# GpSimd takes 48 of the low-part subtractions from VectorE in a transformer block on one core

## Chip, cores and metric

The kernel runs on one core of one Trainium2 chip. The metric is the device time of one execution in microseconds (us); three executions were timed and the median is quoted. A further execution was taken with the hardware profiler, and all rows below come from it.

## What is computed

One block of a streaming encoder for 512 tokens of width 2048, in float32. The first half is attention (latent attention and stick-breaking attention, merged by gates). The second half, where the change lies, is an expert retrieval:

```
h  = rmsnorm(x) * (1 + scale) + shift                 # 512 x 2048
q  = (h @ w_q) -> 8 heads x 256                       # query weights
s1, s2 = q's two halves against 128 keys each
v1, i1 = top_k(s1, 16);  v2, i2 = top_k(s2, 16)       # per head
sc, ci = top_k(v1[i] + v2[j], 16)                     # of 256 pairs
idx = e1 * 128 + e2;  g = softmax(sc)                 # 16 experts a head
act = gelu(h . u_tab[idx]);  y = sum(g * act * v_tab[idx])
x  = x + gate * y
```

## The kernel before, in words

**Split products.** TensorE multiplies in a reduced float32 format (fp32r). To keep accuracy, each weight tile of 128x1024 is split by the helper hl (line 100): the tile raw is loaded on SyncE's queue, ScalarE copies it to hi in fp32r (line 110), VectorE forms lo = raw - hi (line 111), and mm3 (line 124) makes three products, hi*hi (line 125), hi*lo of the activations (line 126) and lo*hi (line 127). There are four raw buffers and three each of hi and lo. After the second normalization the flag prio is set (line 772), so that every later call of hl takes the first branch (lines 109 to 111), which gives the two instructions a high priority.

**Order.** The instructions of each engine run in a fixed order, which a planner makes from its own estimate of durations, with the order of the program as priority. Each engine takes its instructions strictly in that order.

**The stage of the change (build3).** The query product goes head by head: wq_part (line 774) makes a quarter of a head's product, so 4 tiles and 96 matmuls a head. Heads 0 and 1 come first (lines 784 to 786 and 900 to 903). Then, for each head, ScalarE copies the product (qT, line 825), TensorE makes the scores (pscore, line 836), ScalarE copies these (s, line 839, four buffers), the product of the next head is issued (wq_mm), and VectorE selects the best keys (topk, line 843): rows of top-8, index and replace operations over 128 and then 256 candidates, small conversions (lines 851, 863, 864, 867), the candidate sums (cand, line 855), then one-hot compares, products and reductions (lines 869 to 871), a difference df (line 873) whose exponential ScalarE takes (line 874), and the weights gn (line 878).

After the heads come 12 chunks of the dense first product of the experts (lead_chunk, line 889, through u_mm, line 880): a chunk is 2 tiles and 48 matmuls of 352 columns into the tile pul, and ScalarE takes a gelu of it (line 893). These do not need the selection. What follows does: the indices (line 936), a rearranged copy h2r with one buffer (line 948) which TensorE transposes (ph2x, line 951), and the transposes of the selected indices and weights (ptr, line 1009). Then 12 further chunks (line 1042) are interleaved with g_batch (line 1018): 44 batches in which VectorE builds one-hot tiles o1 and o2 (lines 1026 and 1028) and TensorE multiplies them (pg, line 1034). From there GpSimd also issues the gathers of expert rows (line 964), and VectorE uses the rows (lines 970 and 982). The rest of the kernel, half of its time, runs the remaining chunks of the first product and the second product (pvv).

GpSimd does nothing else than a few memsets early (line 549) until the writes of g_d (line 1039) and the gathers.

Of the kernel before, what the change touches and what calls it, by code (L numbers as in the profile page):

```python
# [24 lines left out]
NL0 = 12  # L25
# [47 lines left out]
def build(tc, a, dbg=None, upto=99):  # L73
    nc = tc.nc
    VE, SC, GP, TE, SY = nc.vector, nc.scalar, nc.gpsimd, nc.tensor, nc.sync
# [21 lines left out]
    def bank(name="bk"):  # L97
        return ps.tile([128, 512], F32, name=name, tag="ps", bufs=8)

    def hl(src, n=1024, rb=4, sb=3, q=None):  # L100
        raw = st.tile([128, 1024], F32, name="raw", tag="raw", bufs=rb)
        hi = st.tile([128, 1024], F32R, name="hi", tag="hi", bufs=sb)
        lo = st.tile([128, 1024], F32R, name="lo", tag="lo", bufs=sb)
        if q is None:
            SY.dma_start(raw[:, :n], src)
        else:
            q.dma_start(raw[:, :n].rearrange("p (m c) -> p m c", m=src.shape[1]), src)
        if prio[0]:
            with tc.high_priority():
                SC.activation(hi[:, :n], raw[:, :n], AF.Copy)  # L110
                VE.tensor_sub(lo[:, :n], raw[:, :n], hi[:, :n])  # L111
        else:
            SC.activation(hi[:, :n], raw[:, :n], AF.Copy)  # L113
            VE.tensor_sub(lo[:, :n], raw[:, :n], hi[:, :n])  # L114
        return hi, lo
# [163 lines left out]
    def part_mm(src, m0, m1, k0, k1, out, begin, end):  # L279
        nk = k1 - k0  # L280
        pb = {}
        for ma in range(m0, m1, max(1, 8 // nk)):
            mb = min(m1, ma + max(1, 8 // nk))
            parts = -(-nk // 8)
            step = -(-nk // parts)
            for ka in range(k0, k1, step):
                kb = min(k1, ka + step)
                w = kb - ka
                hi, lo = hl(src[ma:mb, :, ka * 128:kb * 128].rearrange("m p c -> p m c"), (mb - ma) * w * 128, q=WQ)
                for m in range(ma, mb):  # L290
                    if ka == k0:
                        pb[m] = begin(m)
                    for k in range(ka, kb):
                        c = ((m - ma) * w + k - ka) * 128
                        mm3(pb[m][:], (hi[:, c:c + 128], lo[:, c:c + 128]), (hT[0][:, k, :], hT[1][:, k, :]),
                            *out(m, k, k0, k1))
                    if kb == k1:
                        end(m, pb[m])
                yield
# [418 lines left out]
def build3(tc, a, dbg, upto, L):  # L718
    nc = tc.nc
    VE, SC, GP, TE, SY = nc.vector, nc.scalar, nc.gpsimd, nc.tensor, nc.sync  # L720
    PO, Hp, st, mg = L["PO"], L["Hp"], L["st"], L["mg"]
    bank, hl, rawload, mm3, dump = L["bank"], L["hl"], L["rawload"], L["mm3"], L["dump"]
# [21 lines left out]
    for d in range(16):  # L744
# [3 lines left out]
        for hf in range(2):  # L748
            hi, lo = hl(a["w_out"][d, hf])
# [22 lines left out]
    L["prio"][0] = True  # L772

    def wq_part(h, pb, kq):
        hi, lo = hl(a["w_q"][h, kq])
        for kk in range(4):
            k = kq * 4 + kk
            for m in range(2):
                o = (m * 4 + kk) * 128
                mm3(pb[m][:], (hi[:, o:o + 128], lo[:, o:o + 128]), (h2[0][:, k, :], h2[1][:, k, :]), k == 0, k == 15)  # L780
# [4 lines left out]
    for h, kq in QORDER:  # L785
        wq_part(h, pq[h], kq)
# [29 lines left out]
    def wq_mm(h):  # L816
        pq[h] = [bank("pwq") for _ in range(2)]
        for kq in range(4):
            wq_part(h, pq[h], kq)
# [59 lines left out]

    def u_mm(e2, pu, step=lambda: None):  # L880
        for hf in range(2):
            hi, lo = hl(a["u_t"][e2, hf])
            for kk in range(8):
                k = hf * 8 + kk
                mm3(pu[:, :TD], (hi[:, kk * 128:kk * 128 + 128], lo[:, kk * 128:kk * 128 + 128]),
                    (h2c[0][:, k, :], h2c[1][:, k, :]), k == 0, k == 15)
            step()

    def lead_chunk(c):
        pu = bank("pul")  # L890
        u_mm(c, pu)
        al = Rp.tile([128, TD], F32, name="al", tag="al", bufs=3)
        SC.activation(al[:], pu[:, :TD], AF.Gelu_apprx_tanh)  # L893
        SC.dma_start(act_d[c], al[:])
# [3 lines left out]
    for h in range(NH):  # L898
        ss = scores(h, wq_evac(h))
        if h == 0:  # L900
            for kq in range(4):
                if (1, kq) not in QORDER:
                    wq_part(1, pq[1], kq)
        elif h + 1 < NH:
            wq_mm(h + 1)
        if h == 0:
            for j in range(4):
                h2f = Qp.tile([128, 4, 128], F32, name="h2f", tag="qT", bufs=3)
                VE.tensor_add(h2f[:], h2[0][:, 4 * j:4 * j + 4, 0:128], h2[1][:, 4 * j:4 * j + 4, 0:128])
                pb = bank("ph2n")  # L910
                for i in range(4):
                    TE.transpose(pb[:, i * 128:i * 128 + 128], h2f[:, i, :], ident)
                SC.activation(h2nat[:, j * 512:j * 512 + 512], pb[:], AF.Copy)
            VE.tensor_add(h2xT[:], h2[0][:, :, 128:T0], h2[1][:, :, 128:T0])
        topk(h, ss)
        if h < 4:
            for j in range(2):
                r = slice(4 * h, 4 * h + 4)
                SC.activation(h2c[j][:, r, :], h2[j][:, r, T0:T], AF.Copy)
# [173 lines left out]
    def u_chunk(e2):  # L1093
        pu = psu.tile([128, 512], F32, name="pu", tag="pu", bufs=2)
        u_mm(e2, pu, sub)
        at = Ep.tile([128, TD], F32, name="at", tag="at", bufs=3)
        SC.activation(at[:], pu[:, :TD], AF.Gelu_apprx_tanh)
        make_w(e2, at)
# [225 lines left out]
```

## Time and profile before

| what | value |
|---|---|
| median of 3 runs | 3744.23 us (3740.5 to 3745.46) |
| the profiled execution | 3744.19 us, of which 3742.4 us from the first to the last instruction |
| TensorE busy | 3636.3 us, 97% of the span |
| VectorE busy | 2843.9 us, 76% |
| ScalarE busy | 1316.7 us, 35% |
| GpSimd busy | 576.1 us, 15% |
| mean granted TensorE clock | 0.990 |

The engines are named PE (TensorE), DVE (VectorE), ACT (ScalarE), POOL (GpSimd) and SP (SyncE). A row of a timeline gives start, duration, engine, line, operation, output and inputs, count, and in brackets the idle time of that engine before it and what ended it. Busy shares are means over stages with different limits, so the stages are read one by one.

### The profile page before, as it was taken

To read this page: it belongs to the slowest core of one execution; us is meant where nothing else is said; L and a number is where in the kernel's file an instruction comes from. 1 tells how busy PE (TensorE), PEld (TensorE's weight loads), DVE (VectorE), ACT (ScalarE), POOL (GpSimd) and SP (SyncE) were. 2 spreads that over 40 slices of the span, in tenths; PEclk is the share of its full clock that TensorE was granted. 3 is DMA by queue.
4 is the path that set the end of the run, shared out by engine and by line. 5 is a ranking of instruction groups with operands and counts; after the bars stand their busy time and mean duration, and the time that the engine had idled before them with its cause. 6 is when DMAs were issued, how large, how long until landed. Compare 5 with 4: busy or idle time off the path is not lost. (4 is left out here: it accounts for less than half of the span.)

```text
span 3742.4 us, 51570 instructions
## 1 busy us (share of the span) xinstructions
PE 3636.3 (97%) x20173; PEld 3280.9 (88%) x20173; DVE 2843.9 (76%) x4261; ACT 1316.7 (35%) x1775; POOL 576.1 (15%) x367
## 2 busy tenths in 40 slices
PE   8999999999999989998899999999999999999998
PEld 4776778888788878798899999999999999999988
DVE  6857665555344349999988888888898988889876
ACT  3243335555422233234333333333333333333333
POOL 0000000000000000001123333333333324232200
PEclk9999999999999999999999999999999999999999
DMA  8746655544444432245789999999999999999974
GB/s 299 256 146 211 187 184 164 163 153 155 127 137 141 145 115 89 83 142 212 266 331 343 350 343 348 343 344 342 354 337 342 345 348 347 341 341 350 338 221 124
DMA packets 328388, 926.92 MB, mean 248 GB/s; under 512 B 24360, under 2 KB 96040, under 8 KB 285360
## 3 DMA queue, kind: packets, MB, share of 16 engines
q1 hardware_dynamic: 261424, 539.20, 43.4%
q0 software_dynamic: 47664, 358.63, 25.2%
q10 hardware_dynamic: 19056, 25.79, 1.9%
q8 instruction: 158, 2.59, 0.3%
q14 instruction: 86, 0.70, 0.1%
HBM read 878.53 MB, written 44.97 MB: 247 GB/s over the span
## 5 line engine op out<-in xcount | busy, mean ns | idle before, releaser
L125 PE MATMUL pvv<-wh,hi 128*128 128x352 f32 x2048 | 660.2, 322 | 9.5 <-DVE acc L1128 9.4
L126 PE MATMUL pvv<-wl,hi 128*128 128x352 f32 x2048 | 662.4, 323 | 0.0
L127 PE MATMUL pvv<-wh,lo 128*128 128x352 f32 x2048 | 661.9, 323 | 0.0
L126 PE MATMUL pu<-h2c_lo,hi 128*128 128x352 f32 x1664 | 540.5, 325 | 0.0
L127 PE MATMUL pu<-h2c_hi,lo 128*128 128x352 f32 x1664 | 537.3, 323 | 0.0
L125 PE MATMUL pu<-h2c_hi,hi 128*128 128x352 f32 x1664 | 534.7, 321 | 1.3 <-ACT al L893 1.3
L110 ACT ACTIVATE hi<-raw 128x1024 fp32r<-128x1024 f32 x288 | 304.2, 1058 | 506.0 <-PE pu L126 273.5
L1223 ACT ACTIVATE hi<-raw 128x1024 fp32r<-128x1024 f32 x256 | 271.9, 1062 | 593.5 <-PE pvv L126 307.2
L964 POOL DMA_INDIRECT gt<-in_u,idx x128 | 218.5, 1707 | 1639.7 <-PE pg L1034 1223.1
L113 ACT ACTIVATE hi<-raw 128x1024 fp32r<-128x1024 f32 (+2 forms) x193 | 201.8, 1046 | 590.2 <-PE proj L126 177.4
L125 PEld LDWEIGHTS pvv<-wh,hi 128*128 128x128 f32 x2048 | 385.6, 188 | 13.0 <-DVE acc L1128 9.2
L111 DVE TENSOR_TENSOR lo<-raw,hi 128x1024 fp32r<-128x1024 f32 x288 | 351.4, 1220 | 57.1 <-ACT hi L110 55.9
L127 PEld LDWEIGHTS pvv<-wh,lo 128*128 128x128 f32 x2048 | 385.9, 188 | 1.1 <-issue 0.8
L126 PEld LDWEIGHTS pvv<-wl,hi 128*128 128x128 f32 x2048 | 385.6, 188 | 0.0
L114 DVE TENSOR_TENSOR lo<-raw,hi 128x1024 fp32r<-128x1024 f32 (+2 forms) x193 | 232.7, 1206 | 156.3 <-ACT hi L113 149.8
L982 DVE SCALAR_TENSOR_TENSOR ghA<-gt,wk,ghA 128x2048 f32<-128x2048 f32 x127 | 298.1, 2348 | 50.8 <-DMA gt<-in_v,idx 50.4
L1224 DVE TENSOR_TENSOR lo<-raw,hi 128x1024 fp32r<-128x1024 f32 x256 | 312.1, 1219 | 22.4 <-ACT hi L1223 21.7
L970 DVE SCALAR_TENSOR_TENSOR gt<-gt,h2nat 128x2048 f32<-128x2048 f32 x128 | 292.5, 2286 | 37.4 <-DMA gt<-in_u,idx 37.0
L125 PEld LDWEIGHTS pu<-h2c_hi,hi 128*128 128x128 f32 x1664 | 312.3, 188 | 1.6 <-ACT al L893 1.6
L127 PEld LDWEIGHTS pu<-h2c_hi,lo 128*128 128x128 f32 x1664 | 312.7, 188 | 0.0
L126 PEld LDWEIGHTS pu<-h2c_lo,hi 128*128 128x128 f32 x1664 | 312.3, 188 | 0.0
L964 POOL DMA_INDIRECT gt<-in_v,idx x128 | 229.1, 1790 | 457.0 <-PE pu L127 188.1
(334 smaller groups left out, 6905.5 us busy)
## 6 DMA issues: line engine op xcount, KB each, us to landing
raw<-in_u_t SPq DMA_DIRECT2D x256, 512.0 KB
raw<-in_v SPq DMA_DIRECT2D x256, 512.0 KB
raw<-in_ada SPq DMA_DIRECT2D x128, 512.0 KB
araw<-in_ada SPq DMA_DIRECT2D x64, 512.0 KB
raw<-in_w_gate SPq DMA_DIRECT2D x44, 512.0 KB
g_d<-stg POOLq DMA_DIRECT2D x11, 2048.0 KB
gg<-g_d SPq DMA_DIRECT2D x32, 704.0 KB
raw<-in_w_out SPq DMA_DIRECT2D x32, 512.0 KB
```

Source lines behind the costliest of these rows:

```text
L110: SC.activation(hi[:, :n], raw[:, :n], AF.Copy)
L111: VE.tensor_sub(lo[:, :n], raw[:, :n], hi[:, :n])
L113: SC.activation(hi[:, :n], raw[:, :n], AF.Copy)
L114: VE.tensor_sub(lo[:, :n], raw[:, :n], hi[:, :n])
L125: TE.matmul(out, w[0], x[0], start=first, stop=False, **kw)
L126: TE.matmul(out, w[0], x[1], start=False, stop=False, **kw)
L127: last_mm[0] = TE.matmul(out, w[1], x[0], start=False, stop=last, **kw)
L964: ins = GP.indirect_dma_start(out=t[:], out_offset=None, in_=a[tab], in_offset=bass.IndirectOffsetOnAxis(ap=ix[:, k:k + 1], axis=0))
L970: pace(VE.scalar_tensor_tensor(t[:], t[:], 1.0, h[:], op0=ALU.mult, op1=ALU.mult, accum_out=dt[:, k:k + 1]), mybir.DependencyClass.NoSync)
L982: ins = VE.scalar_tensor_tensor(accs[tag][:], t[:], w[:, k:k + 1], accs[tag][:], op0=ALU.mult, op1=ALU.add)
L1223: SC.activation(hi[:], raw[:], AF.Copy)
L1224: VE.tensor_sub(lo[:], raw[:], hi[:])
```

## The change

The helper hl gets an argument sub, the engine that makes lo in its high-priority branch. GpSimd makes it for the query weights of heads 2 to 7 (6 heads of 4 tiles) and for the first 12 chunks of the first product (12 chunks of 2 tiles): 48 subtractions of 128x1024. All others stay on VectorE.

```diff
-    def hl(src, n=1024, rb=4, sb=3, q=None):
+    def hl(src, n=1024, rb=4, sb=3, q=None, sub=None):
...
         if prio[0]:
             with tc.high_priority():
                 SC.activation(hi[:, :n], raw[:, :n], AF.Copy)
-                VE.tensor_sub(lo[:, :n], raw[:, :n], hi[:, :n])
+                (sub or VE).tensor_sub(lo[:, :n], raw[:, :n], hi[:, :n])
...
     def wq_part(h, pb, kq):
-        hi, lo = hl(a["w_q"][h, kq])
+        hi, lo = hl(a["w_q"][h, kq], sub=GP if h > 1 else None)
...
     def u_mm(e2, pu, step=lambda: None):
         for hf in range(2):
-            hi, lo = hl(a["u_t"][e2, hf])
+            hi, lo = hl(a["u_t"][e2, hf], sub=GP if e2 < NL0 else None)
```

NL0 is 12 (line 25).

## Rows read from the trace of the kernel before

**Rows 1.** Busy time by stage; the columns are named in its first line.

```profile
core 0: us, PE busy (x) PEld busy (x) DVE busy (x) ACT busy (x) POOL busy (x), PEclk, DMA share, GB/s
...
1460.00:1680.00 220.00, 212.06 (x1107) 186.20 (x1106) 219.97 (x877) 69.19 (x88) 0.00 (x0) 1.00 0.34 108
...
1700.00:1720.00 20.00, 18.75 (x112) 17.77 (x113) 13.96 (x32) 8.32 (x15) 1.07 (x1) 0.80 0.31 101
1740.00:1900.00 160.00, 141.43 (x1011) 137.77 (x1011) 160.00 (x366) 64.42 (x100) 23.07 (x21) 1.00 0.71 267
1950.00:2000.00 50.00, 50.00 (x314) 50.00 (x313) 40.95 (x41) 20.49 (x26) 20.26 (x10) 1.00 0.96 362
2000.00:3700.00 1700.00, 1687.29 (x10457) 1680.51 (x10456) 1487.25 (x1388) 556.67 (x669) 514.23 (x288) 1.00 0.92 332
```

**Rows 2.** Waits, 1449 to 1725 us: total us, times, longest us.

```profile
ACT df L874 <- DVE df L873: 40.2, 7, 10.3
...
PE ph2x L951 <- DVE h2r L948: 5.9, 4, 4.3
PE pul L127 <- DVE lo L111: 5.0, 7, 1.8
```

**Rows 3.** VectorE groups, 1449 to 1697 us: shapes, count, busy us, mean ns.

```profile
L111 DVE TENSOR_TENSOR lo<-raw,hi 128x1024 fp32r<-128x1024 f32 x47 | 57.0, 1214 | 0.6 <-ACT hi L110 0.6
L869 DVE TENSOR_TENSOR oh<-cf,iota 128x1024 f32<-128x1024 f32 x16 | 19.5, 1217 | 0.0
...
L851 DVE CAST ft<-ix 128x16 f32<-128x16 uint32 x56 | 9.3, 166 | 0.0
L855 DVE TENSOR_TENSOR cand<-vt 128x1024 f32<-128x1024 f32 x7 | 8.5, 1211 | 0.0
```

**Rows 4.** Timeline of TensorE, 1514 to 1519 us and 1590 to 1724 us.

```profile
1517.55 1.16 PE L836 MATMUL pscore<-ky,qT 128*128 128x128 f32 x8 [2.13 <-ACT qT L825]
...
1593.04 0.41 PE L125 MATMUL pul<-h2c_hi,hi 128*128 128x352 f32 x1
...
1698.42 1.11 PE L951 MATMUL ph2x<-cst,h2r 128*128 128x128 f32 x4 [4.34 <-DVE h2r L948]
...
1706.02 0.64 PE L125 MATMUL pul<-h2c_hi,hi 128*128 128x352 f32 x1
...
1714.68 3.73 PE L1034 MATMUL pg<-o,o 128*128 128x128 f32 x32
```

**Rows 5.** Timeline of VectorE, 1685 to 1698 us.

```profile
1692.62 1.22 DVE L111 TENSOR_TENSOR lo<-raw,hi 128x1024 fp32r<-128x1024 f32 x1
1693.76 1.22 DVE L870 TENSOR_TENSOR oh<-oh,ft 128x1024 f32<-128x1024 f32 x1
...
1697.28 0.22 DVE L878 TENSOR_TENSOR gn<-df,sm 128x64 f32<-128x64 f32 x1
```

**Rows 6.** Timeline of GpSimd, 0 to 1720 us.

```profile
0.25 0.10 POOL L1315 MEMSET const-float32-0.0<- 128x1 f32 x1 [0.25 <-issue]
...
545.34 0.14 POOL L549 MEMSET pr<- 64x64 f32 x1 [8.21 <-PE ppt L562]
1718.10 1.07 POOL L964 DMA_INDIRECT gt<-in_u,idx  x1 [1172.61 <-PE pg L1034]
```

**Rows 7.** Timelines of GpSimd and VectorE, 2032 to 2062 us.

```profile
2033.42 0.93 POOL L964 DMA_INDIRECT gt<-in_u,idx  x1 [1.48 <-PE pvv L127]
...
2032.63 0.88 DVE L1128 TENSOR_TENSOR acc<-acc,pvv 128x704 f32<-128x704 f32 x1
...
2056.56 1.87 POOL L964 DMA_INDIRECT gt<-in_u,idx  x1 [1.48 <-PE pu L127]
...
2055.34 2.28 DVE L970 SCALAR_TENSOR_TENSOR gt<-gt,h2nat 128x2048 f32<-128x2048 f32 x1
```

**Rows 8.** VectorE groups by shape, 0 to 40 us.

```profile
L250 DVE SCALAR_TENSOR_TENSOR ang<-nn,ang 128x512 f32<-128x512 f32 x3 | 2.1, 692 | 0.1
...
L245 DVE CAST ang<-posi 128x512 f32<-128x512 int32 x1 | 0.4, 429 | 8.4 <-DMA posi<-in_pos 8.4
```

## The prediction

> **What bounds the kernel now.** I first read the busy time by stage [rows 1]. From 2000 to 3700 us TensorE is busy 1687 of 1700 us; nothing in that half depends on the change, so a shift that reaches 1908 us, where this part begins, is carried to the end. The stage of the change is different: from 1460 to 1680 us VectorE is busy 219.97 of 220 us and TensorE 212.06, and from 1740 to 1900 VectorE is busy 160.00 of 160 and TensorE 141.43. So the expert selection and the one-hot batches are bound by VectorE, and TensorE waits here and there. Next the waits [rows 2]: ScalarE stands 40.2 us for the difference df of the selection, and as it works in order, the hi tiles queue behind it; TensorE loses 5.0 us on late lo tiles and 5.9 us on h2r. The VectorE groups say what fills it [rows 3]: 47 of the subtractions at issue lie between 1449 and 1697 us. Last the timelines: the selection of head 7 ends at 1697.5 us [rows 5], and TensorE, done with chunk 11, has stood 4.34 us for it [rows 4]. The clock is 0.80 of full speed from 1700 to 1720 us [rows 1], after that idle time: part of that stretch ran at 1.2 GHz and not 2.4.
>
> **What is removed.** The 48 subtractions are 24 for six heads and 24 for twelve chunks. Of the 47 in that window, 45 are moved ones (two belong to chunk 12; three moved ones lie earlier). One lasts 1.21 us [rows 3] but overlaps the next operation: the one that began at 1692.62 was followed at 1693.76 [rows 5], a step of 1.13 to 1.14 us. So 45 x 1.13 = 51 us leave VectorE ahead of the end of the selection, which would end at 1697.5 - 51 = 1646 us if nothing else changed.
>
> **What TensorE can do with it.** The order gives TensorE the 12 chunks before ph2x. One chunk is 48 matmuls at 50.00/314 = 0.159 us [rows 1], 7.64 us; twelve are 91.7 us. Chunk 0 started at 1593.04 us [rows 4], and the 2.13 us stand at 1517 us (scores waiting for a copy that ScalarE held behind df [rows 4]) would go, so it starts at 1590.9 and chunk 11 ends at 1682.6 us. Then h2r is long ready, and ph2x starts at 1682.6 + about 1 us instead of 1698.42: 14.8 us earlier. The three shorter stands in ph2x stay, as h2r has one buffer. Chunk 12 took 1714.68 - 1706.02 = 8.66 us [rows 4], 1.0 over the 7.64 of full clock; without idle time before it, that comes back. The most that the change can bring is thus 15.8 us, far less than the 51 us of VectorE work (I assume that the planner keeps this order of the stages): from 1646 to 1683 us VectorE would stand idle, as everything after needs the transposes behind chunk 11. The later start of the batches is carried on one for one, since VectorE is full from there to 1900 us and its work there is unchanged.
>
> **What GpSimd adds.** GpSimd's queue is empty from 545.34 to 1718.10 us [rows 6], so the subtractions delay nothing on it as long as they end before the first gather. No row shows a subtraction on GpSimd. The lower end is VectorE's 1.21 us. The nearest rows of GpSimd itself are memsets: 0.10 us for 1 element a partition and 0.14 for 64 [rows 6], so 1024 cost some 0.65 us a stream, and two inputs and an output one after another 2.0 us. I take 2.0. The upper end is the pace at which TensorE uses a tile, 24 x 0.159 = 3.8 us in a chunk; above it GpSimd would set the pace. The Trainium skill ("GPSIMD Engine Reference", section "Elementwise — side-by-side cycle accounting") gives 4497 ns for 2048 elements; half of that, an estimate of 2.25 us, would not change the forecast.
>
> At 2.0 us lo comes 0.8 us later behind hi. The three buffers let hi run two tiles ahead, 7.6 us, which covers that; where ScalarE was held by df, it is not covered. So I leave 3 us of TensorE's 5.0 us of waits for lo in place. The raw buffer is released 0.8 us later too, so SyncE's next load on its queue starts that much later; four buffers are 15 us of tiles, and the DMA share is 0.34 here [rows 1], so I cost that at nothing; without that cover it would be at most 48 x 0.8 = 38 us.
>
> **The two engines hold each other.** While VectorE ran an operation with two inputs in SBUF (line 970, 2055.34 to 2057.62 us), a descriptor operation of GpSimd that began at 2056.56 ended at 2058.43, 0.81 us after it; one that began during an operation with one input in PSUM (line 1128) took its usual 0.93 us [rows 7]. So GpSimd waits for the whole of a two-input operation. The reverse, VectorE waiting for a GpSimd operation that reads two tiles, no row shows: its price lies between 0 and the whole 48 x 2.0 = 96 us. The 248 us of the window hold 7 selections (7 cand [rows 3]) and 53 us of subtractions, so one selection is some 27 us. In it cand and four one-hot operations have two inputs (line 869 twice [rows 3], line 870 as often): cand alone (1.1 us), the others, with two reductions, in a stretch of an estimated 7.3 us. A GpSimd operation of 2.0 us meets the first with (1.1 + 2.0)/27 and the second with (7.3 + 2.0)/27, together 46% of the time, so 22 of 48; a meeting costs between half and the whole of 2.0 us, I take 1.4: 31 us. The selection then ends at 1646 + 31 = 1677 us, still ahead of TensorE's 1683.
>
> **Sum.** 14.8 + 1.0 - 3 = 12.8 us; I take 2 us off for ph2x meeting a selection that ends with little to spare: 11 us. Against the profiled execution of 3744.19 us (it agrees with the median of 3744.23) this gives **3733 us**.
>
> **The rivals.**
> *No hold at all* on VectorE: the full 15.8 us and perhaps 1 us of waits more, 3727 us. Against it stands the hold in the other direction [rows 7].
> *Slower: the small conversions are held too.* A CAST of 512 elements takes 0.429 us where a two-input operation takes 0.692 [rows 8], so VectorE runs such one-input operations at about twice the rate, and they may need the path that GpSimd uses. With 56 casts [rows 3], about as many shifts, masks and the two-input ones (some 175 in 195 us without the subtractions), an operation that can be held comes every 1.1 us, so nearly each GpSimd operation stops VectorE once, for 2.0 - 0.55 = 1.45 us: 48 x 1.45 = 70 us added where 51 to 53 were taken. The selection ends some 17 us later, at 1715, and the VectorE-bound batches with it; less a little filling by TensorE, 3759 us. It decides from 1.13 us of hold per operation on. The Trainium skill says just this ("SBUF — State Buffer", section "Who interferes with whom"): copies, casts and tensor_scalar in two-port modes, and two-input operations, contend with GpSimd, and the loser is blocked for the whole instruction. By that rule the time is that of this rival; the trace agrees for two-input operations only.
> *Same: the hold is about as large as the saving,* 1.0 to 1.25 us per operation (some conversions held, or a longer GpSimd operation): the selection ends within 6 us of 1697, 3744 us.
> *GpSimd sets the pace:* at 4.5 us a subtraction, 24 x (4.5 - 3.8) = 17 us of chunks and more hold, 3765 us.
> That the change does nothing can be left out: line 772 sets prio before any of the calls.
>
> **Chances.** Forecast 0.40, no hold 0.08, same 0.20, conversions held 0.27, GpSimd as the pace 0.05. About 0.2% (7.5 us) can be told from no change; so faster 0.48, same 0.20, slower 0.32. The range reaches from 3727 (no hold) to 3762 (conversions held, with 2.1 us per operation); the forecast's own range is 3728 to 3738.
>
> **What would show it.** In the new profile: 48 rows of line 111 on POOL and 48 fewer on DVE; their duration against 2.0 and 3.8 us; the mean of lines 869 and 855 above 1.21 us (two-input operations held) and of lines 851, 863 and 864 above 0.17 (conversions held); the start of ph2x against 1698.42, and what ended the idle time before it. The prediction is wrong if ph2x starts later than 1698, or if it starts 12 us earlier and the end does not follow.

## The result and the profile after

The changed kernel takes 3789.31 us (median; 3787.93 to 3793.6) beside 3742.36 us for the kernel before in the same comparison: 47 us or 1.3% longer, ratio 1.0127 [1.0116, 1.0139]. The forecast was 3733 us; its sign is wrong, and the range ended at 3762. The profiled execution spans 3791.8 us. One execution of e5 (11837 us) and one of the kernel before beside e10 and e11 (6070 us) stood far off all others and are left out of every median below.

The busy time by stage comes first, of the changed kernel, with the columns in its first line.

```profile
core 0: us, PE busy (x) PEld busy (x) DVE busy (x) ACT busy (x) POOL busy (x), PEclk, DMA share, GB/s
1460.00:1680.00 220.00, 181.92 (x829) 151.03 (x828) 219.79 (x812) 47.68 (x65) 81.99 (x30) 0.90 0.25 77
1500.00:1520.00 20.00, 15.73 (x70) 12.66 (x68) 19.97 (x105) 0.00 (x0) 0.97 (x1) 0.98 0.11 34
1540.00:1560.00 20.00, 12.59 (x52) 9.66 (x51) 19.96 (x96) 3.10 (x4) 3.14 (x2) 0.83 0.01 1
1640.00:1660.00 20.00, 11.45 (x61) 10.70 (x60) 19.97 (x85) 4.95 (x6) 4.92 (x2) 0.81 0.08 20
```

Set the first stretch against the same one of before [rows 1]. VectorE is as full as it was (219.79 of 220), although 51 us of work were taken from it. TensorE lost 30 us of work (181.92 against 212.06), and its granted clock fell from 1.00 to 0.90. From 1500 to 1520 us ScalarE did nothing at all, and the DMA share sank to 0.11.

The waits of the changed kernel from 1449 to 1760 us say who stopped TensorE (total us, times, longest).

```profile
ACT df L874 <- DVE df L873: 117.7, 8, 21.0
...
PE pwq L125 <- ACT hi L110: 21.1, 4, 6.5
...
PE pul L125 <- ACT hi L110: 11.1, 2, 6.8
...
PE pwq L127 <- POOL lo L111: 6.7, 4, 2.0
...
PE pul L127 <- POOL lo L111: 3.8, 3, 1.8
...
PE ph2x L951 <- DVE h2r L948: 2.1, 3, 1.0
```

ScalarE's wait for df grew from 40.2 to 117.7 us [rows 2]. TensorE now waits 32.2 us for hi tiles, a row that did not stand among its waits before, and 10.5 us for lo. Its 4.3 us stand ahead of ph2x is gone, as forecast, but not for the forecast's reason (see below). One of ScalarE's stands is seen in the timelines, first of ScalarE:

```profile
1499.40 0.60 ACT L839 ACTIVATE s<-pscore 128x512 f32<-128x512 f32 x1 [0.76 <-PE pscore L836]
...
1520.38 0.26 ACT L874 ACTIVATE df<-df 128x64 f32<-128x64 f32 x1 [20.38 <-DVE df L873]
1520.54 2.94 ACT L110 ACTIVATE hi<-raw 128x1024 fp32r<-128x1024 f32 x3
```

TensorE, the same stand and then the start of ph2x:

```profile
1521.63 0.80 PE L125 MATMUL pwq<-h_hi,hi 128*128 128x512 f32 x1 [5.90 <-ACT hi L110]
...
1751.13 0.60 PE L951 MATMUL ph2x<-cst,h2r 128*128 128x128 f32 x4
```

Having copied the scores, ScalarE goes straight to the exponential of df and stands 20.38 us for it. Three hi tiles follow at once, so nothing but their place in the order had held them. TensorE has run dry meanwhile. In the order of ScalarE's instructions the number of hi tiles that precede the exponentials of heads 0 to 7 was 12, 17, 22, 27, 31, 38, 47, 55; it is now 11, 15, 19, 23, 27, 31, 35, 42. TensorE's order is unchanged.

GpSimd's subtractions in the view by source line (shortest, median and longest in ns, first and last start):

```profile
L111 POOL TENSOR_TENSOR lo<-raw,hi x48: 2344/2408/3427, 1424.0 to 1740.8; 128x1024 fp32r<-128x1024 f32 x48
```

The VectorE groups of the changed kernel from 1449 to 1740 us (count, busy us, mean ns):

```profile
L870 DVE TENSOR_TENSOR oh<-oh,ft 128x1024 f32<-128x1024 f32 x16 | 36.5, 2278 | 0.0
L869 DVE TENSOR_TENSOR oh<-cf,iota 128x1024 f32<-128x1024 f32 x16 | 22.8, 1427 | 0.0
L851 DVE CAST ft<-ix 128x16 f32<-128x16 uint32 x56 | 21.0, 375 | 0.0
L867 DVE CAST cf<-cj 128x64 f32<-128x64 int32 x8 | 16.7, 2087 | 0.0
...
L855 DVE TENSOR_TENSOR cand<-vt 128x1024 f32<-128x1024 f32 x7 | 10.6, 1520 | 0.0
L871 DVE TENSOR_REDUCE e1n<-oh 128x64 f32<-128x1024 f32 x8 | 9.6, 1206 | 0.0
...
L863 DVE TENSOR_SCALAR ci<-ix 128x16 int32<-128x16 int32 x30 | 4.8, 161 | 0.0
```

All 48 are on GpSimd, at 2.41 us each (median). Beside them VectorE's own instructions got longer: line 869 from 1217 to 1427 ns, line 851 from 166 to 375, line 855 from 1211 to 1520 [rows 3]. The reduction of line 871 did not, nor did the shifts of line 863 in this kernel (168 to 161 ns).

How the two engines hold each other stands in their timelines; here the rows of both in turn:

```profile
1485.59 1.21 DVE L869 TENSOR_TENSOR oh<-cf,iota 128x1024 f32<-128x1024 f32 x1
1486.35 2.71 POOL L111 TENSOR_TENSOR lo<-raw,hi 128x1024 fp32r<-128x1024 f32 x1 [10.66 <-ACT hi L110]
1487.05 3.09 DVE L870 TENSOR_TENSOR oh<-oh,ft 128x1024 f32<-128x1024 f32 x1
1489.02 3.38 POOL L111 TENSOR_TENSOR lo<-raw,hi 128x1024 fp32r<-128x1024 f32 x1
1490.07 2.39 DVE L867 CAST cf<-cj 128x64 f32<-128x64 int32 x1
```

Whichever begins second ends a fixed time behind the first: the first subtraction 2.26 us behind line 869, line 870 then 1.08 us behind that subtraction, the second subtraction 2.26 us behind line 870, and the cast 0.06 us behind the second subtraction. So each waited for the other's end and then did its own work. The whole trace of the changed kernel agrees: 36 instructions of VectorE were lengthened, each by a different subtraction. They end 0.03 to 0.14 us behind it (casts and other small ones), 0.55 (the one of 512 elements) or 1.08 to 1.09 us (two inputs of 1024 elements). All 17 subtractions longer than 2.5 us began during line 869 or 870 and end 2.21 to 2.28 us behind it. The last ten of the 48 subtractions began after the selection had ended.

The end of the selection came later in spite of the work taken away: its last reduction ended at 1705.3 us, where gn, the last of it before, ended at 1697.5 [rows 5].

Where the time arose, by the start of TensorE's stages: the first chunk at 1636.47 us (1593.04 before [rows 4]), ph2x at 1751.13 (1698.42), pg at 1765.7 (1714.68). So 43.4 us are lost beside the heads and 9.3 more in the chunks. The spans differ by 49.4 us.

### The profile page after: what moved, and what is told of

It is laid out like the page before. It is cut to its first block, busy times and chain, and to the rows that moved or that the text cites. A ratio compares the mean times of both kernels' runs of the same rounds, so it can differ in the third digit from the quotient of the medians.

```text
span 3791.8 us, 51564 instructions
## 1 busy us (share of the span) xinstructions
PE 3648.1 (96%) x20173; PEld 3289.2 (87%) x20173; DVE 2854.4 (75%) x4213; ACT 1309.1 (35%) x1771; POOL 670.7 (18%) x415
## 5 line engine op out<-in xcount | busy, mean ns | idle before, releaser
L111 DVE TENSOR_TENSOR lo<-raw,hi 128x1024 fp32r<-128x1024 f32 x240 | 293.0, 1221 | 87.1 <-ACT hi L110 86.5
L1224 DVE TENSOR_TENSOR lo<-raw,hi 128x1024 fp32r<-128x1024 f32 x256 | 311.9, 1218 | 24.4 <-ACT hi L1223 23.9
L111 POOL TENSOR_TENSOR lo<-raw,hi 128x1024 fp32r<-128x1024 f32 x48 | 125.3, 2622 | 1072.1 <-ACT hi L110 1069.1
```

The costliest lines, as they stand in the source:

```text
L111: (sub or VE).tensor_sub(lo[:, :n], raw[:, :n], hi[:, :n])
L1224: VE.tensor_sub(lo[:], raw[:], hi[:])
```

## The experiments

Two theories were tried against each other. **Order** (theory A of the expectations): ScalarE's new order costs the time. **Hold** (theory B): a GpSimd subtraction stops VectorE for longer than the 1.13 us that it takes off it. The edits shift line numbers by a few lines: line 111 is line 113 or 117 in some rows below. An order is given by a dependency without a semaphore. The kernel before took 3740.9 us (median) beside e1 to e4, 3739.5 beside e5 to e8, 3740.1 beside e9 and 3741.1 beside e10 and e11.

### e1: the new order alone, without GpSimd

```diff
+    def order_after(ins, first):
+        tc.add_manual_dep(ins.ins, first.ins.name, mybir.DependencyInfo(mybir.DependencyClass.NoSync,
+                              mybir.DependencyReason.DATA), reason="order")
...
-                SC.activation(hi[:, :n], raw[:, :n], AF.Copy)
+                hins.append(SC.activation(hi[:, :n], raw[:, :n], AF.Copy))
+                if len(hins) - 1 in ahead:
+                    order_after(hins[-1], ahead[len(hins) - 1])
...
-        SC.activation(df[:], df[:], AF.Exp)
+        ahead[[11, 15, 19, 23, 27, 31, 35, 42][h]] = SC.activation(df[:], df[:], AF.Exp)
```

> No GpSimd subtraction at all: the kernel before, with one thing changed, that the difference df of each head goes through ScalarE ahead of the hi tiles that it precedes in the changed kernel (df of head h ahead of hi tile 11+4h, where the kernel before had one to thirteen more hi tiles first). Theory A (ScalarE's new order is the cause: the hi tiles stand behind df, TensorE behind them): 3775 to 3800 us, chunk 0 starts near 1630 us. Theory B (the holds between GpSimd and VectorE are the cause): 3744 plus or minus 8 us.

3776.08 us, ratio 1.0096 [1.0079, 1.0113], in the range of theory A. Waits from 1400 to 1760 us:

```profile
ACT df L882 <- DVE df L881: 105.6, 8, 20.0
...
PE pwq L132 <- ACT hi L110: 20.3, 4, 5.5
...
PE pul L132 <- ACT hi L110: 12.8, 2, 8.9
```

These are the waits of the changed kernel, in a kernel whose subtractions are all on VectorE. The order by itself costs 35 us (3776.1 against 3740.9).

### e2: GpSimd with the exponential at the place it had before

The difference is kept in gn, and exponential, sum, reciprocal and product are issued later, behind the hi tiles that preceded them in the kernel before.

```diff
-        SC.activation(df[:], df[:], AF.Exp)
...
+    def finish_ready():
+        while todo and len(hins) > LATE[todo[0]]:
+            h = todo.pop(0)
+            g = gn[:, :, h * 16:h * 16 + 16]
+            order_after(SC.activation(g, g, AF.Exp), hins[LATE[h]])
...
+            VE.tensor_tensor(g, g, sm[:, :, None].to_broadcast([128, 4, 16]), op=ALU.mult)
```

LATE is 11, 16, 21, 26, 30, 37, 46, 54.

> All 48 GpSimd subtractions stay, but df of each head goes through ScalarE at the place among the hi tiles that it has in the kernel before (the exponential and the three small VectorE operations behind it are issued later; df is kept in gn). Theory A: 3735 to 3755 us, since the holds about replace the work that left VectorE. Theory B: 3780 to 3795 us, as the changed kernel.

3778.11 us, ratio 1.0102 [1.0085, 1.0118], in neither range. The first chunk starts at 1597.3 us and not at 1636.5: beside the heads the order was the cause. But 35.5 us are lost behind it, by the waits of e2:

```profile
PE pul L132 <- ACT hi L110: 35.5, 1, 35.5
```

What ScalarE waited for, in its timeline:

```profile
1677.93 1.06 ACT L110 ACTIVATE hi<-raw 128x1024 fp32r<-128x1024 f32 x1 [44.67 <-DMA raw<-in_u_t]
```

And the timeline of SyncE's queue:

```profile
1598.64 25.89 SPq L105 DMA_DIRECT2D raw<-in_u_t  x5
1673.45 0.51 SPq L963 DMA_DIRECT2D g0x<-gn  x1
1674.05 12.40 SPq L105 DMA_DIRECT2D raw<-in_u_t  x7
```

SyncE's queue stood for a small copy of gn, which the deferral makes late, with the raw loads behind it. So this run has a fault of its own, and e5 takes it away.

### e3 and e4: half of the change each

```diff
-            hi, lo = hl(a["u_t"][e2, hf], sub=GP if e2 < NL0 else None)
+            hi, lo = hl(a["u_t"][e2, hf], sub=None)
```

for e3 (GpSimd for heads 2 to 7 alone), and for e4 (the 12 chunks alone) the same in wq_part.

> GpSimd makes lo for heads 2 to 7 only; the 12 chunks go back to VectorE. The order of df among the hi tiles is that of the changed kernel for heads 0 to 5. Theory A: nearly the whole loss, 3775 to 3795 us. Theory B: half of the subtractions, half of the loss, 3760 to 3772 us.

> GpSimd makes lo for the 12 chunks only; heads 2 to 7 go back to VectorE. The order of df among the hi tiles is that of the kernel before for heads 0 to 4 and two to six tiles earlier for heads 5 to 7. Theory A: 3740 to 3758 us. Theory B: half of the loss, 3760 to 3772 us.

e3: 3778.31 us, 1.0088 [1.0069, 1.0108]. e4: 3759.57 us, 1.0043 [1.0027, 1.006]. The planner gave e3 nearly the changed kernel's order (11, 15, 19, 23, 27, 31, 37, 46), with df waits of 103.0 us. It gave e4 the order of before up to head 4, and then 36, 42, 49. So e3 came out as theory A has it, and e4 at the edge between the two ranges. The waits of e4:

```profile
ACT df L874 <- DVE df L873: 62.6, 7, 16.7
PE pul L125 <- ACT hi L110: 19.5, 3, 8.7
```

So the waits for hi move to where the order moved, in e4 to the chunks. The order follows the subtractions that the planner sees leave VectorE. That its estimate, without the hold, is the reason is argued from this, not shown.

### e5 and e6: order and SyncE's queue put right, with GpSimd and without

```diff
+            r_ = SY.dma_start(raw[:, :n], src)
+            raws.append(r_)
...
-        SY.dma_start(g0x[q * XT:q * XT + XT, :], gn[0:XT, 1, q * XT:q * XT + XT])
+        r_ = SY.dma_start(g0x[q * XT:q * XT + XT, :], gn[0:XT, 1, q * XT:q * XT + XT])
+        order_after(r_, raws[55])
```

(the copies into idxx likewise), on top of e2; e6 has all subtractions on VectorE.

> As e2 (48 GpSimd subtractions, df at its place in the kernel before), and on SyncE's queue the eight small copies of the indices and weights (lines 943 and 944 of the kernel before) go behind the raw load of the last of the 12 chunks, so that raw loads no longer queue behind a weight that is finished late. Theory A (the order on the in-order queues is the cause): 3735 to 3755 us. Theory B (the holds cost the time whatever the order): 3765 to 3785 us.

> Control of e5: the same edits with all subtractions on VectorE. Both theories: as the kernel before, 3738 to 3748 us. Its difference to e5 is what the 48 subtractions on GpSimd cost or bring at an equal order: Theory A within 10 us, Theory B e5 longer by 20 us or more.

e5: 3756.9 us, 1.0049 [1.0033, 1.0065], between the two ranges. e6: 3739.62 us, 1.0006 [0.9997, 1.0016]. So the edits cost nothing, and with the same order of exponentials and hi tiles the 48 subtractions on GpSimd cost 17 us. VectorE's own order is not the same in the two kernels, as the planner interleaves the heads anew, but VectorE is busy 219.86 and 220.00 of 220 us there (1460 to 1680), so the sum of its work decides, and that is taken below. The VectorE groups of e5, 1449 to 1740 us:

```profile
L883 DVE TENSOR_TENSOR oh<-oh,ft 128x1024 f32<-128x1024 f32 x16 | 35.4, 2210 | 0.1
L864 DVE CAST ft<-ix 128x16 f32<-128x16 uint32 x56 | 29.3, 523 | 0.0
...
L868 DVE TENSOR_TENSOR cand<-vt 128x1024 f32<-128x1024 f32 x7 | 16.5, 2351 | 0.0
```

### e7 and e8: all exponentials behind the last hi tile of chunk 11

LATE is 55 for every head; ScalarE then never stands for df while TensorE needs a hi tile. e7 is with GpSimd, e8 without.

> As e5, but df of all heads in one place, behind the hi tile of the last of the 12 chunks: no hi tile ever queues behind a selection (the copies s of the scores still can). Theory A: 3730 to 3748 us, chunk 0 starts near 1593 us. Theory B: 3760 us or more.

> As e7 with all subtractions on VectorE. Both theories: 3732 to 3746 us, as TensorE's 7 us of waits behind df may go, and the end of the selection stays where it is. Theory A expects e7 within 10 us of it.

e7: 3759.52 us, 1.0048 [1.0032, 1.0063]. e8: 3741.14 us, 1.0003 [0.9993, 1.0012]; the difference is 18.4 us. e8 is in its range, e7 at the lower bound of theory B's. In e7 the loss has gathered in one stand, as the waits of e7 from 1449 to 1760 us show:

```profile
PE ph2x L977 <- DVE h2r L974: 20.6, 4, 19.0
```

The same row of e8:

```profile
PE ph2x L977 <- DVE h2r L974: 7.0, 4, 5.4
```

The busy time of e7 in the stage of the stand:

```profile
1700.00:1720.00 20.00, 4.39 (x17) 3.19 (x18) 17.23 (x47) 7.09 (x10) 0.00 (x0) 0.50 0.24 73
```

VectorE is the last here: ph2x starts at 1714.05 us against 1695.1 in e8.

### e9: as e7, with GpSimd for the 24 tiles of the chunks alone

The edit of e3 made in wq_part, on top of e7.

> As e7 (all eight exponentials behind the hi tile of chunk 11, small copies of SyncE behind the raw load 55), but GpSimd makes lo for the 12 chunks alone: 24 subtractions instead of 48. The edits without GpSimd (e8) gave the time of the kernel before, 3741 us. If the cost at an equal order is a hold per GpSimd subtraction (e7 less e8: 18.4 us for 48, after what the removal gives back), 24 of them cost half: some 9 us, 3750 us, mean of the one-hot products (oh from oh and ft) near 1.8 us and of CAST ft near 0.35. If what costs is the start of the held stretch or a single bad meeting, whatever the count, it stays at some 3759; if only the subtractions beside the heads hold VectorE, it is 3741.

3745.14 us, 1.0016 [1.0007, 1.0025]: 5 us over before and 4 over e8 for 24 subtractions, where 9 were expected and e7 has 18 for 48. Oh from oh and ft took 1468 ns in the mean, CAST ft 421. At the start of ph2x the profiled executions of e9 and e7 are 7.8 and 18.9 us behind e8's, so where the loss arises, half the subtractions cost about two fifths. Of the 24, 19 held an instruction of VectorE. e4, with the same 24, costs some 14 us more, and differs in the order.

### e10 and e11: the small conversions batched, with GpSimd and without

```diff
+            ix = Qp.tile([128, 4, 16], U32, name="ix", tag="ix", bufs=2)
             for tb in range(4):
...
-                VE.tensor_copy(ft[:, tb, :], ix[:])
+            VE.tensor_copy(ft[:], ix[:])
...
-            VE.tensor_scalar(ci[:, tb, :], ix[:].bitcast(I32), 4, None, op0=ALU.arith_shift_right)
+        VE.tensor_scalar(ci[:], ix[:].bitcast(I32), 4, None, op0=ALU.arith_shift_right)
```

(cj likewise), on top of e5 and e6. A head then has 2 casts ft of 64 elements in place of 8 of 16, and one shift and one mask in place of 4 each.

> e5 (48 GpSimd subtractions, exponential at the place of before, SyncE order mended: 3759 us, ph2x at 1711.5) with the small conversions of the selection batched: the 8 CAST ft of 16 elements a head become 2 of 64, the 4 shifts ci and 4 masks cj become 1 each. So VectorE has 12 fewer instructions a head, of some 0.09 us from start to start, 9 us over the 8 heads, and three quarters of the conversions that a GpSimd subtraction can hold are gone. If the hold falls on an instruction of the held kinds wherever one is met (conversions, two-input operations), and a subtraction beside the top-8 searches costs nothing, the hold on CAST ft (25 us) and on ci (9 us) falls to a quarter, 26 us less, with the 9 us removed 35: the selection would end near 1680, ph2x is then bound by TensorE's chunks near 1692, and the time is 3736 to 3742, no slower than the control e11 by more than 4 us. If a subtraction is simply held over to the next two-input operation, so that each of the 48 still costs its 1.5 us, only the 9 us are won: 3750.

> The control of e10: the same batched conversions with all subtractions on VectorE (e6 with them batched). 96 instructions fewer of some 0.09 us from start to start, 9 us of VectorE ahead of the end of the selection; TensorE's chunks end near 1682, so ph2x starts some 4 to 8 us earlier than in e6 (1694.8): 3732 to 3737 us. If VectorE was not what ended last, 3740.

e10: **3730.27 us**, 0.9974 [0.9964, 0.9983], 6 us under its range. e11: 3734.70 us, 0.9985 [0.9976, 0.9994], in its range. Each against the kernel before beside it, batching is worth 28 us with GpSimd (from 17.4 over, e5, to 10.8 under) and 6.5 us without (from 0.1 over, e6, to 6.4 under). The busy time of e10 in the stage:

```profile
1460.00:1680.00 220.00, 218.21 (x1151) 194.41 (x1150) 218.85 (x781) 71.40 (x92) 114.81 (x44) 1.00 0.34 114
```

The start of ph2x in TensorE's timeline of e10:

```profile
1687.61 0.60 PE L978 MATMUL ph2x<-cst,h2r 128*128 128x128 f32 x4
```

Two VectorE groups of e10, 1449 to 1740 us:

```profile
L884 DVE TENSOR_TENSOR oh<-oh,ft 128x1024 f32<-128x1024 f32 x16 | 31.4, 1965 | 0.1
...
L864 DVE CAST ft<-ix 128x64 f32<-128x64 uint32 x14 | 7.0, 497 | 0.0
```

TensorE is busy 218.21 of 220 us and goes into ph2x without a wait, so the selection is off the path. Casts are still held (497 ns on average, where the same casts take 179 to 211 in e11), but there are 14 and not 56. The product of line 884 is no longer than its 2210 ns in e5, and all two-input rows together are held no more than there (28.9 against 29.8 us in the sums below), so the hold was not merely put off to the next two-input operation. The subtractions that held an instruction are 27 of 48, after 44 in e5.

e10 is faster than the kernel before (by 11 us) and than the changed kernel. Against e11, its mean over eleven executions is 3.7 us lower, with a 95% interval of about 0.8 to 6.5 us by their scatter: probably a gain, of a tenth of a percent. The profiled execution of e11 was the fastest of its eleven and that of e10 one of the slower ones, so their spans (3728.9 and 3732.2 us) do not tell. The stages show where it comes from: e10's first chunk starts 5.6 us later than e11's, but its chunks take 92.9 us up to ph2x where e11's take 102.1, with 6.4 us of waits for VectorE's lo.

### The sums

VectorE's time from one start to the next was added up from 1417 us to about the end of the last selection, by kind of instruction, and each kernel with GpSimd set against the one without.

| us | before to changed | e6 to e5 | e8 to e7 | e11 to e10 |
|---|---|---|---|---|
| lo, 47 to 51 fewer | -57.8 | -56.5 | -52.8 | -54.3 |
| one-hot (oh) | +20.5 | +19.6 | +22.8 | +17.5 |
| casts ft | +16.2 | +24.2 | +25.4 | +5.3 |
| casts cf | +15.2 | +8.7 | +4.4 | +6.7 |
| shifts ci, masks cj | 0.0 | +3.9 | +11.5 | 0.0 |
| cand, gn | +8.8 | +10.2 | +6.4 | +11.4 |
| other held rows | +4.1 | +1.9 | +1.9 | +2.7 |
| held in all | +64.8 | +68.5 | +72.4 | +43.6 |
| per GpSimd subtraction (by 48) | 1.35 | 1.43 | 1.51 | 0.91 |
| subtractions that held an instruction | 36 | 44 | 45 | 27 |

At 1.13 us removed for each, the first three lose and the last gains. The net sums, +7.0, +12.0, +19.6 and -10.7 us, follow the shift of the end of the last selection: +9.0, +16.2, +19.2 and -9.7 us. In the changed kernel that is the smaller part: the selection ends 9.0 us later, and ph2x starts 52.7 us later.

| kernel | us | first chunk | ph2x | pu |
|---|---|---|---|---|
| before | 3742.36 | 1593.0 | 1698.4 | 1909.5 |
| changed | 3789.31 | 1636.5 | 1751.1 | 1960.6 |
| e1 order alone | 3776.08 | 1617.7 | 1732.5 | 1940.5 |
| e5 GpSimd, order kept | 3756.9 | 1598.2 | 1711.5 | 1922.8 |
| e6 its control | 3739.62 | 1589.6 | 1694.8 | 1905.9 |
| e7 GpSimd, exponentials last | 3759.52 | 1595.4 | 1714.1 | 1924.9 |
| e8 its control | 3741.14 | 1587.2 | 1695.1 | 1905.8 |
| e9 as e7, 24 tiles | 3745.14 | 1592.4 | 1702.9 | 1913.4 |
| e10 GpSimd, batched | 3730.27 | 1594.7 | 1687.6 | 1897.2 |
| e11 its control | 3734.70 | 1589.2 | 1691.3 | 1899.3 |

(us, and the start of stages in us in the profiled execution; pu is the tile of the first product in the second half of the kernel. From the start of pu to the end the profiled executions took between 1829.6 and 1836.5 us, in no order of the edits, so that a difference of a few us is better read from the stage starts.)

## Why the prediction was wrong

- **The step that failed first** is "I assume that the planner keeps this order of the stages". TensorE's order was kept, ScalarE's was not: each exponential came ahead of the next hi tiles. The text had seen that "the hi tiles queue behind it", left 3 us of waits for lo in place for it, and put a change of ScalarE's order at nothing, without a reason. It cost 30 us: the changed kernel is 47.0 us over the kernel before beside it, and e5, where GpSimd has the same work and the order is mended, 17.4. The order alone costs 35 us (e1), and order and hold do not simply add up (35 + 17 = 52 against 47).
- **The mis-sized term** is the hold, taken as 31 us for 22 of 48 meetings. It came to 68.5 and 72.4 us with ScalarE's order mended (e5, e7), by 44 and 45 meetings of about 1.6 us each. So the price of a meeting (1.4 us) was near, and the count was half. The meetings had been counted against two-input operations alone, but casts of 16 elements, and in e5 and e7 shifts or masks, are held too, and there are 18 of these in each head. With the hold at 31 us the selection was to end at 1677 us; it ended at 1708.8 in e5. This step alone turns the forecast's gain into a loss of 17 us.
- **The rival "the small conversions are held too"** was right in mechanism, and in size partly by luck: 1.45 us a subtraction, 70 us in all, 3759 us. e5 and e7 gave 1.43 and 1.51, 68.5 and 72.4, 3756.9 and 3759.5. But its 1.45 us was 2.0 less 0.55; with the 2.41 us that a subtraction took, it would have been 1.86 us and 89 us. Its sign would have been right; it did not have the order either. The Trainium skill's rule that spoke for it ("SBUF — State Buffer", section "Who interferes with whom") has the engine that comes second blocked for the whole instruction, and reductions never in contention. The trace agrees: with the casts, the two-input rows and the shifts of e7 (474 ns), and with the reduction of line 871, which stayed at 1206 ns.
- **Right:** the 48 rows on GpSimd; a subtraction below TensorE's pace of 3.8 us; the later shift carried to the end (51.1 us at pu, 49.4 at the end). The 91.7 us of twelve chunks, and about 1 us to ph2x, are what TensorE reaches without waits: 92.9 us in e10, where the kernel before took 101.0 us up to its stand (1593.04 to 1694.08). The 4.3 us stand ahead of ph2x is gone by luck: the selection ended later and not earlier, and TensorE got there 57 us later.
- **The price on GpSimd** was taken as 2.0 us and measured 2.41. The estimate from the Trainium skill ("GPSIMD Engine Reference", section "Elementwise — side-by-side cycle accounting"), 2.25 us, was nearer.
- **"From 1646 to 1683 us VectorE would stand idle"** was never reached in the changed kernel: it is full there. It came true in a smaller measure in e10, where VectorE first stands idle for more than a moment at the chunks' end, from 1680.7 us. That e10 gains the forecast's 11 us is chance: 6 of them e11 has without GpSimd.
- **The clock** is part of the loss: TensorE's granted clock is 0.83 and 0.81 in stretches behind a stand (first profile above), where it was 1.00 before. These are parts of the stretch at 1.2 GHz and not 2.4. How much of the 47 us this makes up, no run separates.

## What to carry to other kernels

When a change makes one engine's list shorter, compare the order of every in-order engine before any sum: here the engine that lost the time (ScalarE) was not touched by the diff. Count each instruction of VectorE that a two-input GpSimd operation can hold, the tiny ones above all, because such a meeting costs up to a whole GpSimd operation whatever the size of the held instruction (up to 2.25 us here). If the work is to move, batch the small conversions first: the same move cost 17 us with 23 such instructions a head (casts, shifts, masks, cand, oh), and with 11 it brought some 4 us.

## What the runs showed of the hardware

A cast of 16 elements, which takes 0.143 to 0.189 us in the kernel before, took up to 2.392 us beside GpSimd's subtractions: as long as one of them (median 2.408), at whose end it waited. Reductions of 1024 elements (1206 ns) and top-8 searches were not lengthened, beside 82 us of GpSimd work in 220.

A GpSimd subtraction of 128x1024 takes twice VectorE's 1.21 us, and in the changed kernel up to 3.43 us. The long ones are the hold in the other direction [rows 7]: all 17 over 2.5 us began during a two-input operation of VectorE and ended 2.21 to 2.28 us behind it.

TensorE's granted clock was 0.50 (1.2 GHz throughout) from 1700 to 1720 us in e7, where it worked 4.39 of 20 us, most of the rest being the stand of 19 us.
